# Two transformer blocks in one launch: the Pool engine's two-operand elementwise work moved to VectorE

## Chip, cores and metric

One core of one Trainium2 chip. The metric is the device time of one execution in microseconds (us). Engines are named as the profile names them: PE is TensorE (PEld its weight loads), DVE is VectorE (`V` in the code), ACT is ScalarE (`S`), POOL is GpSimd (`G`, called Pool), SP issues most DMAs.

## The reference

512 tokens of 1024 features in float32 go through two blocks. In outline, cut to what matters (helper functions, reshapes and some arguments are left out):

```python
def first_block(x, mem, ...):
    h = rms_norm(x, norm_mix_pre)
    q_d, k_d, v_d, u_p, q_m, gate_logits = split(h @ w_in)
    y_attn = rms_norm(diff_attention(q_d, k_d, v_d, lam), subln_g) * 0.8 @ w_attn_branch   # 8 heads
    y_pool = multiscale_pool(u_p, ...) @ w_pool_branch    # trailing means over 2, 4, 8, 16 tokens
    y_mem = memory_cross_attention(q_m, rms_norm(mem) @ w_mem_kv) @ w_mem_branch            # 4 heads
    g = sigmoid(gate_logits)
    x = x + rms_norm((g[0] * y_attn + g[1] * y_pool + g[2] * y_mem) @ w_out, norm_mix_post)
    up = causal_depthwise_conv(rms_norm(x, norm_ffn_pre) @ w_up)                            # 3 taps
    return x + rms_norm((gelu(up_g) * up_v) @ w_down, norm_ffn_post)

def second_block(x, c, ctx, c_ctx, ...):                  # 2 layers, context of 256 tokens
    for i in range(2):
        h_lat, h_ctx = (rms_norm(t) * (1 + scale) + shift for t in (x_lat, x_ctx))
        if i == 0:   # attention with rotated, normed heads | attention in a window of 128 with a sink
            y_lat, y_ctx = even_mixer(h_lat, h_ctx, ...)
        else:        # convolution of 31 taps over 512 channels, layer norm | neighbourhood attention, 8 heads
            y_lat, _ = odd_mixer(h_lat, h_ctx, ...)
        x_lat = x_lat + g_l * y_lat                       # and the context in layer 0
    return rms_norm(x_lat, final_g)
```

The change touches the elementwise work around these products: squares for norms, splits of operands, the sums of pool windows and branches, rotations, gates, and the 31-tap convolution of layer 1.

## The kernel before

**Layout.** Activations stand as [128 features, tokens], eight blocks of 512 tokens for the 1024 features. Weights come from memory as tiles `raw` of 128 output features × 1024, two ahead.

**Products.** A float32 product is made of three passes of a reduced type (`mm3`, recorded as L294): high part by high part, high by low, low by high. So each operand needs two parts. For weights `Product.parts` makes them: ACT copies `raw` to `whi` (L458), another engine subtracts, `wlo = raw - whi` (L460). Which engine that is stands in the list `lo_engines`: VectorE, but Pool after `low_parts_on(G)`, which is called at the start (until the first products) and before layer 0's attention. For activations `split` does the same (L489, L490).

**Order.** TensorE works in program order. Products stand in batches; `weave` places steps of a batch between the steps of an attention, `advance` between blocks of a norm. `defer(us, f)` runs f after so many microseconds of products. The list `background` holds work of other engines; `rate[0]` of it is emitted for each microsecond of products, 0.85 in layer 1. The order of the other engines' queues is made by a scheduler from the order of the program and its dependences; each engine works through its queue in order.

**Pool's work before.** Two-operand work: the low parts of weights (above); in `SumSq(..., True)` every third block's square, into an accumulator of its own; in `norm_to` the low part of each block with k % 3 == 1; in `pool_sums` the doubling sums of the windows (L717); in `next_branch` the sum of the mix (L851); in `rotary` two of four products (L1068, L1070); in `post_norm` six of eight x += y (L1418); in `lat_apply` the product by the gate (L1517) and seven of eight splits; in `layer_norm` two sums (L1731, L1732); at the end three of eight last scalings. One-operand work: the scaling of the probabilities by 1/l (L775, L921, L1131), the negation of biases (L1648), fills.

**The convolution of layer 1.** For each of four blocks of channels, `value` forms `up` and puts 32 steps on `background`. Tap 0 is an ACT activation with the bias. Taps 1 to 17 are one VectorE instruction each (L1710), `u = up[j:] * w[j] + u`. The last 13 (`NTAP`) are an ACT activation each that scales (L1713, L1716), and for 12 of them a Pool addition into `ub` (L1717). VectorE adds `ub` to `u` at the end (L1723). The steps of the two kinds alternate. While they run, TensorE works through layer 1's 32 attention steps (`na_items`): scores, minimum (L1122), exponential on ACT (L1126), 1/l on VectorE (L1130), scaling on Pool (L1131), transposes (L586), split on ACT and VectorE (`pth`, `ptl`), output sums (L1163). Products of the next convolution, of attention and of gates are woven in. The layer norm follows the last tap (`layer_norm`: sums over channels, L1736, centring L1741, squares, scaling), beside the products of the gates; the output products follow it.

**Layer 0's attention.** 16 heads of 4 steps, in the same form; in it `lat_apply` applies the gates to finished blocks.

**Norm boundaries.** `post_norm` adds the normed output to x (L1417, L1418) and sums x's squares (L552); `token_sums` makes one matmul for each 128 tokens and accumulator, and `rsqrt` (L524 to L532) works on VectorE.

Of the kernel before, what the change touches and what calls it, by code (L numbers as in the profile page):

```python
# [18 lines left out]
P = 128  # L19
T = 512  # L20
# [4 lines left out]
NTA = 5     # scratch tiles  # L25
NTG = 4     # scratch tiles of the products' results
NRAW = 2    # weight tiles as loaded
NW = 2      # weight tiles in parts
NPT = 1     # transposed probabilities
NSB = {2: 3, 5: 3, 6: 3}     # scores, by the blocks of keys  # L30
NOT = 1     # one half of an attention output
NTAP = 13   # convolution taps on the Pool engine
TH = 3      # last products that take all tokens at once
LL, LN = 2, 2                # heads' scores ahead: latents of layer 0, layer 1

# microseconds of products, or steps of them, before or between other work
SM, SX, SA = 2.4, 4, 8       # start: the memory's root, the input's squares, the input's root
PD = 16                      # multiscale pool
DA, DR, DG = 36, 2.4, 3.7    # differential attention: ahead, for each step, root
B1A = 4                      # second norm of a boundary between layers  # L40
RG = 3.5                     # rotation
MB, CR, MR = 15, 5.4, 0.15   # context: modulation blocks before it, steps, rate of the modulation after it
LA, LR, LZ = 16, 0.5, 1.0    # latents of layer 0: ahead, for each step, fewer after a product
NR = 1.85                    # layer 1: for each step
TD = 2.5                     # last norm

# ---------------------------------------------------------------- host layout
# [135 lines left out]
# ---------------------------------------------------------------- program  # L183


class X:
    """A moving operand in two parts: h and l are [128, kt, n] float32r tiles."""
# [5 lines left out]
class Blocks:  # L193
    """[128, kt, n] as a tile for each of the kt blocks"""
# [8 lines left out]
def body(nc, tc, A, out, dbg=None):  # L203
# [21 lines left out]
    def set_banks(mm, tr, scores=True):  # L225
        """the banks for the products' results and for those of attention and of statistics; scores take four others"""
# [49 lines left out]
    rate = [0.0, 0.0]  # L276
    count = [0]
    woven = []
    lo_engines = deque()

    def low_parts_on(*engines):
        lo_engines.clear()
        lo_engines.extend(engines)
# [1531 lines left out]
```

## Time and profile before

| | |
|---|---|
| three runs | 1807.56, 1810.9, 1818.63 us, median 1810.9 |
| profiled execution, its span | 1808.9 us, 25065 instructions |
| PE busy | 1684.3 us, 93% |
| DVE busy | 1278.4 us, 71%, x2474 |
| ACT busy | 902.7 us, 50% |
| POOL busy | 390.0 us, 22%, x364 |

The profile gives no other time of its execution than the span; it is 2.0 us under the median of the runs. Busy times are shares of that span, and a mean over stages of very different kind: up to 62 us norms and first weights, to 465 the branches' inputs and the two attentions of block 1, to 662 the mix, its output product and the first norm boundary, to 1094 the feed-forward (with the context's attention), to 1150 the second boundary, from 1225 to 1415 layer 0's attention, from 1500 to 1712 layer 1, then the output products and the last norm.

### The profile page before, as it was taken

The page shows a single profiled execution, that of the slowest core. Times are in us where ns is not written, and L with a number is a line of the kernel's source. Part 1 is how long each engine was busy: PE and PEld are TensorE (multiplying, and loading weights), DVE is VectorE, ACT ScalarE, POOL GpSimd, SP SyncE. Part 2 cuts the span into 40 slices and gives each one's busy share as a digit, 9 for nine tenths or more (in the row PEclk, how much of TensorE's full clock was granted, in tenths as well). Part 3 has the DMA queues.
Part 4 walks back from the last instruction along what each step waited for, and adds up shares of the span by engine and source line. Part 5 has one row for each costly group of instructions (what it writes and reads, how often), then busy time and mean ns, then how long its engine had stood idle before and what let it go on. Part 6 is the DMA issues. An engine that isn't in the chain of part 4 may idle for free. (4 is left out here: it accounts for less than half of the span.)

```text
span 1808.9 us, 25065 instructions
## 1 busy us (share of the span) xinstructions
PE 1684.3 (93%) x8756; PEld 1407.0 (78%) x8756; DVE 1278.4 (71%) x2474; ACT 902.7 (50%) x1700; POOL 390.0 (22%) x364
## 2 busy tenths in 40 slices
PE   7899999999998889999999998999988989888797
PEld 7788888888776768888778777778877787777677
DVE  6678766777597676644664767677778667888774
ACT  5443225555423456654763433366767445565452
POOL 3320111010021210000000002145544004656400
PEclk8999999999999999999999999999999999999898
DMA  5435555544364432333333556232321554243141
GB/s 197 136 121 176 162 164 151 135 122 117 126 202 161 148 103 94 123 118 105 111 100 110 193 163 211 84 103 70 78 64 47 186 172 137 82 120 97 35 140 59
DMA packets 84878, 227.10 MB, mean 126 GB/s; under 512 B 12048, under 2 KB 24720, under 8 KB 84752
## 3 DMA queue, kind: packets, MB, share of 16 engines
q1 hardware_dynamic: 82880, 220.51, 39.3%
q10 hardware_dynamic: 1872, 4.98, 0.9%
q8 instruction: 70, 1.15, 0.3%
q14 instruction: 56, 0.46, 0.1%
HBM read 181.93 MB, written 9.44 MB: 106 GB/s over the span
## 5 line engine op out<-in xcount | busy, mean ns | idle before, releaser
L294 PE MATMUL mm<-hh,whi 128*128 128x512 f32 (+1 forms) x1120 | 442.2, 395 | 16.6 <-DVE tg L593 4.6
L458 ACT CAST whi<-raw 128x1024 fp32r<-128x1024 f32 (+2 forms) x264 | 268.4, 1017 | 378.7 <-PE mm L294 326.8
L294 PE MATMUL mm<-hh,wlo 128*128 128x512 f32 (+1 forms) x1120 | 424.1, 379 | 6.4 <-DVE wlo L460 6.4
L294 PE MATMUL mm<-hl,whi 128*128 128x512 f32 (+1 forms) x1120 | 424.5, 379 | 3.4 <-DVE hl L490 1.7
L460 DVE TENSOR_TENSOR wlo<-raw,whi 128x1024 fp32r<-128x1024 f32 (+2 forms) x245 | 309.9, 1265 | 151.1 <-ACT whi L458 147.2
L294 PEld LDWEIGHTS mm<-hh,whi 128*128 128x128 f32 x1120 | 216.6, 193 | 51.4 <-DVE tg L593 6.1
L294 PEld LDWEIGHTS mm<-hh,wlo 128*128 128x128 f32 x1120 | 215.2, 192 | 48.8 <-DVE wlo L460 7.8
L294 PEld LDWEIGHTS mm<-hl,whi 128*128 128x128 f32 x1120 | 216.3, 193 | 34.2 <-DVE hl L997 2.7
L1131 POOL TENSOR_SCALAR sb<-sb,l 128x256 f32<-128x256 f32 (+3 forms) x128 | 106.3, 832 | 453.8 <-DVE l L1130 377.6
L294 PE MATMUL mm<-h2h,whi 128*128 128x512 f32 x352 | 141.8, 403 | 4.0 <-DVE cv L1342 3.0
L490 DVE TENSOR_TENSOR ptl<-tr,pth 128x512 fp32r<-128x512 f32 (+2 forms) x240 | 115.6, 497 | 41.8 <-ACT pth L489 40.0
L489 ACT CAST pth<-tr 128x512 fp32r<-128x512 f32 (+2 forms) x240 | 100.3, 436 | 89.8 <-PE tr L586 88.3
L294 PE MATMUL mm<-h2l,whi 128*128 128x512 f32 x352 | 140.1, 398 | 3.5 <-POOL h2l L490 2.1
L294 PE MATMUL mm<-h2h,wlo 128*128 128x512 f32 x352 | 139.7, 397 | 0.8 <-DVE wlo L460 0.8
L586 PE MATMUL tr<-c,sb 128*128 128x128 f32 x624 | 107.5, 282 | 25.1 <-DVE ptl L490 12.8
L586 PEld LDWEIGHTS tr<-c,sb 128*128 128x128 f32 x624 | 78.9, 145 | 52.0 <-issue 10.3
L810 DVE CUSTOM_DVE_ANT_0 mj<-mraw,cb 128x1024 f32<-128x1024 f32 x88 | 111.1, 1263 | 1.2 <-DMA mraw<-in_mod_w 0.5
L1126 ACT ACTIVATE sb<-sb,mn 128x512 f32<-128x512 f32 (+1 forms) x64 | 49.7, 776 | 70.7 <-DVE mn L1122 51.6
L1710 DVE SCALAR_TENSOR_TENSOR mixf<-up,vec,mixf 128x512 f32<-128x512 f32 x68 | 80.9, 1189 | 1.0 <-ACT mixf L1708 0.2
L294 PEld LDWEIGHTS mm<-h2l,whi 128*128 128x128 f32 x352 | 66.4, 189 | 19.2 <-POOL h2l L490 3.2
L294 PEld LDWEIGHTS mm<-h2h,whi 128*128 128x128 f32 x352 | 66.3, 188 | 19.2 <-issue 4.0
L1717 POOL TENSOR_TENSOR ub<-ub,ta 128x512 f32<-128x512 f32 x48 | 78.9, 1644 | 7.8 <-ACT ta L1716 5.1
(374 smaller groups left out, 3303.6 us busy)
## 6 DMA issues: line engine op xcount, KB each, us to landing
raw<-in_w_in SPq DMA_DIRECT2D x56, 512.0 KB, 3.4
mraw<-in_mod_w SPq DMA_DIRECT2D x48, 512.0 KB, 3.4
raw<-in_w_up SPq DMA_DIRECT2D x44, 512.0 KB, 3.4
raw<-in_ev_w SPq DMA_DIRECT2D x40, 512.0 KB, 3.4
raw<-in_od_w SPq DMA_DIRECT2D x36, 512.0 KB, 3.5
qd<-hl SPq DMA_DIRECT2D x48, 256.0 KB, 5.1
raw<-in_w_d SPq DMA_DIRECT2D x16, 512.0 KB, 3.3
raw<-in_ev_o SPq DMA_DIRECT2D x16, 512.0 KB, 3.4
```

The source lines that it names most:

```text
L294: on_pe(nc.tensor.matmul(ps, l, r, start=start, stop=stop), max(n * 0.00042, 0.107) * (2 if l.dtype == F32 else 1))
L458: S.copy(out=self.hi[:, :n], in_=self.raw[:, :n])
L460: lo_engines[-1].tensor_tensor(out=self.lo[:, :n], in0=self.raw[:, :n], in1=f32(self.hi[:, :n]), op=ALU.subtract)
L489: S.copy(out=hi, in_=src)
L490: (eng or V).tensor_tensor(out=lo, in0=src, in1=f32(hi), op=ALU.subtract)
L586: on_pe(nc.tensor.transpose(out=ps[:, k * P:(k + 1) * P], in_=src(b), identity=ident), 0.107)
L810: tc.keep_in_program_order(V.tensor_tensor_reduce(out=jk, in0=raw, in1=cb[:, n, :], scale=0.5, scalar=0.0, op0=ALU.mult, op1=ALU.add, accu ...
L1126: S.activation(out=sb, in_=src, func=AF.Exp, scale=-1.0, bias=mn, accum_out=l[:, 0:1])
L1131: G.tensor_scalar(out=sb, in0=sb, scalar1=l[:, 0:1], scalar2=0.0, op0=ALU.mult, op1=ALU.add)
L1710: V.scalar_tensor_tensor(out=u[m], in0=up[:, j:j + T], scalar=wc(j), in1=u[m], op0=ALU.mult, op1=ALU.add)
L1717: G.tensor_tensor(out=st["ub"], in0=st["ub"], in1=pj, op=ALU.add)
```

## The change

All two-operand work named above is written for VectorE. Pool keeps the scalings, negations and fills, and gets the copies of at most 8 columns at the head of the pool sums. `SumSq` has one accumulator, so `token_sums` makes four matmuls fewer in each of three norms. The convolution has 30 taps on VectorE for each block of channels (tap 0 stays on ACT), no `ub`, no closing addition, and 31 steps instead of 32 on `background`. At the end the copy of r on ACT goes. Comments go as well, so lines have other numbers after the change (L1710 is L1694, L460 is L451, L490 is L481, L1131 is L1117).

```diff
-                lo_engines.rotate(-1)
-                lo_engines[-1].tensor_tensor(out=self.lo[:, :n], in0=self.raw[:, :n], in1=f32(self.hi[:, :n]), op=ALU.subtract)
+                V.tensor_tensor(out=self.lo[:, :n], in0=self.raw[:, :n], in1=f32(self.hi[:, :n]), op=ALU.subtract)
...
-    def split(src, hi, lo, eng=None):
+    def split(src, hi, lo):
         S.copy(out=hi, in_=src)
-        (eng or V).tensor_tensor(out=lo, in0=src, in1=f32(hi), op=ALU.subtract)
+        V.tensor_tensor(out=lo, in0=src, in1=f32(hi), op=ALU.subtract)
...
-            i = 1 if self.two and self.k % 3 == 2 else 0
-            self.k += 1
-            if i == len(self.accs):
+            if not self.accs:
...
-                (G if i else V).tensor_tensor(out=acc, in0=acc, in1=sq, op=ALU.add)
+                V.tensor_tensor(out=acc, in0=acc, in1=sq, op=ALU.add)
...
-            split(t, dst.h[:, k, :], dst.l[:, k, :], G if k % 3 == 1 else V)
+            split(t, dst.h[:, k, :], dst.l[:, k, :])
...
-    low_parts_on(G)
     advance(filler, SX)
-    ss = SumSq(T, True).add_all(ks(xin))
+    ss = SumSq(T).add_all(ks(xin))
...
-                G.tensor_tensor(out=nx[:, sh:], in0=cur[:, sh:], in1=cur[:, :T - sh], op=ALU.add)
-                V.tensor_copy(out=nx[:, :sh], in_=cur[:, :sh])
+                V.tensor_tensor(out=nx[:, sh:], in0=cur[:, sh:], in1=cur[:, :T - sh], op=ALU.add)
+                G.tensor_copy(out=nx[:, :sh], in_=cur[:, :sh])
...
-        G.tensor_tensor(out=mixacc[:, m, :], in0=mixacc[:, m, :], in1=t, op=ALU.add)
+        V.tensor_tensor(out=mixacc[:, m, :], in0=mixacc[:, m, :], in1=t, op=ALU.add)
...
-                G.tensor_tensor(out=a[1], in0=xf[1], in1=sin, op=ALU.mult)
+                V.tensor_tensor(out=a[1], in0=xf[1], in1=sin, op=ALU.mult)
                 V.tensor_tensor(out=a[2], in0=xf[0], in1=sin, op=ALU.mult)
-                G.tensor_tensor(out=a[3], in0=xf[1], in1=cos, op=ALU.mult)
+                V.tensor_tensor(out=a[3], in0=xf[1], in1=cos, op=ALU.mult)
...
-            (V if k % 4 == 3 else G).tensor_tensor(out=xs[k], in0=xs[k], in1=y[:, k, :], op=ALU.add)
+            V.tensor_tensor(out=xs[k], in0=xs[k], in1=y[:, k, :], op=ALU.add)
...
-        G.tensor_tensor(out=mixf[:, m, :], in0=mixf[:, m, :], in1=sg, op=ALU.mult)
-        defer(2.5, lambda: split(mixf[:, m, :], mix.h[:, m, :], low(m), V if m == 7 else G))
+        V.tensor_tensor(out=mixf[:, m, :], in0=mixf[:, m, :], in1=sg, op=ALU.mult)
+        defer(2.5, lambda: split(mixf[:, m, :], mix.h[:, m, :], low(m)))
...
-    low_parts_on(G)
     set_banks(1, 3)
...
-                elif j < 31 - NTAP:
+                else:
                     V.scalar_tensor_tensor(out=u[m], in0=up[:, j:j + T], scalar=wc(j), in1=u[m], op0=ALU.mult, op1=ALU.add)
-                elif j == 31 - NTAP:
-                    st["ub"] = tl(ep, [P, T], "ub", 1)
-                    S.activation(out=st["ub"], in_=up[:, j:j + T], func=AF.Copy, scale=wc(j))
-                else:
-                    pj = tt()
-                    S.activation(out=pj, in_=up[:, j:j + T], func=AF.Copy, scale=wc(j))
-                    G.tensor_tensor(out=st["ub"], in0=st["ub"], in1=pj, op=ALU.add)
-
-            nv = 31 - NTAP
-            order = [j for a, b in zip(range(nv), chain(range(nv, 31), [None] * 31)) for j in (a, b) if j is not None]
-            order += [j for j in range(31) if j not in order]
-            background.extend([lambda j=j: tap(j) for j in order])
-            background.append(lambda: V.tensor_tensor(out=u[m], in0=u[m], in1=st["ub"], op=ALU.add))
+
+            background.extend([lambda j=j: tap(j) for j in range(31)])
...
-        G.tensor_tensor(out=s1, in0=u[0], in1=u[1], op=ALU.add)
-        G.tensor_tensor(out=s2, in0=u[2], in1=u[3], op=ALU.add)
+        V.tensor_tensor(out=s1, in0=u[0], in1=u[1], op=ALU.add)
+        V.tensor_tensor(out=s2, in0=u[2], in1=u[3], op=ALU.add)
...
-        rs = tl(tmp, [P, T], "sqa", 2)[:, :C]
-        S.copy(out=rs, in_=r)
         for k in range(KD):
             t = tt(C) if k % 2 else tg(C)
-            if k % 3 == 2:
-                G.tensor_tensor(out=t, in0=xs[k][:, cs], in1=rs, op=ALU.mult)
-            else:
-                V.tensor_tensor(out=t, in0=xs[k][:, cs], in1=r, op=ALU.mult)
+            V.tensor_tensor(out=t, in0=xs[k][:, cs], in1=r, op=ALU.mult)
```

Three places show how queues look before and after. Each row is one instruction or several equal ones in a row: line, operation, written tile <- read tiles, shape; tile names are those of the code (`s` scores, `sb` probabilities, `ptl` low part of the transposed ones, `mixf` as target of L1710 or L1694 the convolution's sum).

DVE in layer 1's attention, two steps of one head, before:

```order
L490 TENSOR_TENSOR ptl<-tr,pth 128x128
L1122 ISA sb,mn<-s,nab_13986 128x640
L1122 ISA mn 128x1
L1130 RECIPROCAL l<-l 128x1
L490 TENSOR_TENSOR ptl<-tr,pth 128x2x128 x2
L1122 ISA sb,mn<-s,nab_13986 128x640
L1122 ISA mn 128x1
L1701 SCALAR_TENSOR_TENSOR up<-tg,mm 128x512
```

The same steps after:

```order
L1108 ISA sb,mn<-s,nab_13977 128x640
L1108 ISA mn 128x1
L1694 SCALAR_TENSOR_TENSOR mixf<-up,vec,mixf 128x512
L481 TENSOR_TENSOR ptl<-tr,pth 128x2x128
L1116 RECIPROCAL l<-l 128x1
L1694 SCALAR_TENSOR_TENSOR mixf<-up,vec,mixf 128x512
L481 TENSOR_TENSOR ptl<-tr,pth 128x2x128
L1694 SCALAR_TENSOR_TENSOR mixf<-up,vec,mixf 128x512
L1108 ISA sb,mn<-s,nab_13977 128x640
L1108 ISA mn 128x1
```

Taps now stand between the two splits of a step and between minimum and reciprocal, where none stood. Between the instructions that run from 1517.6 to 1676.4 us in the trace of before stand 96 taps instead of 58.

POOL in layer 0's attention before:

```order
L1131 TENSOR_SCALAR sb<-sb,l 128x512 x2
L1517 TENSOR_TENSOR mixf<-mixf,tg 128x512
L460 TENSOR_TENSOR wlo<-raw,whi 128x1024
L490 TENSOR_TENSOR mixf<-mixf,mixh 128x512
L1131 TENSOR_SCALAR sb<-sb,l 128x640 x2
L1131 TENSOR_SCALAR sb<-sb,l 128x512 x2
```

DVE at the same work after (Pool's queue there holds L1117 alone):

```order
L1149 TENSOR_TENSOR mixf<-tr,ot 64x256
L1503 TENSOR_TENSOR mixf<-mixf,tg 128x512
L481 TENSOR_TENSOR ptl<-tr,pth 128x4x128
L481 TENSOR_TENSOR ptl<-tr,pth 128x2x128
L1106 TENSOR_REDUCE mn<-s 128x1
L481 TENSOR_TENSOR mixf<-mixf,mixh 128x512
L451 TENSOR_TENSOR wlo<-raw,whi 128x1024
L481 TENSOR_TENSOR ptl<-tr,pth 128x4x128
```

The gate's product (L1517, now L1503), the split of the block and a weight's low part have moved from between the scalings into VectorE's queue, between splits of probabilities and a minimum.

DVE at the end of layer 1's attention before:

```order
L1130 RECIPROCAL l<-l 128x1
L1710 SCALAR_TENSOR_TENSOR mixf<-up,vec,mixf 128x512
L1723 TENSOR_TENSOR mixf<-mixf,ub 128x512
L1163 TENSOR_TENSOR mixf<-tr,ot 64x256
L490 TENSOR_TENSOR ptl<-tr,pth 128x4x128
L490 TENSOR_TENSOR ptl<-tr,pth 128x128
```

The same after:

```order
L1116 RECIPROCAL l<-l 128x1
L1694 SCALAR_TENSOR_TENSOR mixf<-up,vec,mixf 128x512
L451 TENSOR_TENSOR wlo<-raw,whi 128x1024
L1149 TENSOR_TENSOR mixf<-tr,ot 64x256
L1694 SCALAR_TENSOR_TENSOR mixf<-up,vec,mixf 128x512
L481 TENSOR_TENSOR ptl<-tr,pth 128x4x128
L481 TENSOR_TENSOR ptl<-tr,pth 128x128
L1694 SCALAR_TENSOR_TENSOR mixf<-up,vec,mixf 128x512
L481 TENSOR_TENSOR ptl<-tr,pth 128x2x128 x2
L1694 SCALAR_TENSOR_TENSOR mixf<-up,vec,mixf 128x512 x3
L1149 TENSOR_TENSOR mixf<-tr,ot 64x256
L1694 SCALAR_TENSOR_TENSOR mixf<-up,vec,mixf 128x512 x3
```

Before, the last tap stands ahead of the last splits; after, nine taps follow the last reciprocal, and six of them the last splits. The layer norm's sums come behind them.

## Rows read from the trace of the kernel before

`mm`, `tr` and `s` are TensorE's results in PSUM; L294 is the matmul helper, L586 the transpose.

**Rows 1.** the page's head: span; busy time, share of the span and instructions
```profile
span 1808.9 us, 25065 instructions
...
PE 1684.3 (93%) x8756; PEld 1407.0 (78%) x8756; DVE 1278.4 (71%) x2474; ACT 902.7 (50%) x1700; POOL 390.0 (22%) x364
```

**Rows 2.** stages: length, PE, PEld, DVE, ACT, POOL busy (instructions), PEclk, DMA share, GB/s
```profile
0.00:62.00 62.00, 46.23 (x286) 42.84 (x287) 42.54 (x76) 31.33 (x58) 23.70 (x16) 0.89 0.58 195
62.00:465.00 403.00, 402.94 (x1987) 334.54 (x1986) 290.82 (x680) 175.06 (x381) 58.12 (x66) 1.00 0.46 137
465.00:558.00 93.00, 87.93 (x373) 69.32 (x371) 78.49 (x121) 28.80 (x46) 15.76 (x8) 0.96 0.56 181
600.00:662.00 62.00, 49.76 (x311) 43.59 (x309) 48.55 (x103) 27.58 (x49) 15.15 (x10) 0.92 0.43 138
662.00:1094.00 432.00, 424.12 (x2049) 348.32 (x2050) 261.02 (x437) 232.91 (x371) 16.04 (x32) 1.00 0.38 123
1094.00:1150.00 56.00, 45.87 (x283) 40.14 (x282) 43.06 (x70) 22.21 (x30) 9.81 (x7) 0.94 0.51 176
1225.00:1415.00 190.00, 170.91 (x1061) 147.58 (x1060) 145.69 (x362) 129.46 (x310) 91.80 (x81) 0.97 0.28 77
1517.60:1676.40 158.80, 139.84 (x723) 113.63 (x721) 143.61 (x205) 95.62 (x181) 104.77 (x86) 0.98 0.36 99
1676.40:1712.00 35.60, 25.74 (x128) 21.02 (x128) 30.70 (x63) 19.45 (x43) 15.66 (x12) 0.78 0.12 42
```

**Rows 3.** PE's waits, 1517.6 to 1676.4: us in total, times, longest
```profile
PE tr L294 <- DVE ptl L490: 8.1, 4, 2.4
PE tr L586 <- DVE mixf L1163: 6.7, 4, 2.1
PE tr L586 <- DVE ptl L490: 2.9, 4, 1.2
```

**Rows 4.** chain of waits in 1517.6 to 1676.4, shares by line
```profile
by line: DVE mixf L1710 31.2%; PE mm L294 22.0%; DVE wlo L460 8.1%; issue 7.7%; DVE ptl L490 4.6%; DVE hl L490 4.4%; DVE sb L1122 3.9%; PE tr L586 3.1%; PE tr L294 3.0%; PE s L294 3.0%; ACT whi L458 1.9%; DVE mixf L1163 1.4%; DVE tg L1672 1
```

**Rows 5.** DVE's groups there: line, engine, out<-in, xcount | busy us, mean ns | idle
```profile
L1710 DVE SCALAR_TENSOR_TENSOR mixf<-up,vec,mixf 128x512 f32<-128x512 f32 x58 | 72.0, 1241 | 1.0 <-ACT mixf L1708 0.2
L460 DVE TENSOR_TENSOR wlo<-raw,whi 128x1024 fp32r<-128x1024 f32 x17 | 23.7, 1394 | 1.3 <-ACT whi L458 1.3
...
L490 DVE TENSOR_TENSOR hl<-tg,hl 128x512 fp32r<-128x512 f32 x3 | 5.3, 1770 | 0.0
```

**Rows 6.** timeline of single instructions there: start us, us, engine, line
```profile
1567.39 5.17 DVE L1710 SCALAR_TENSOR_TENSOR mixf<-up,vec,mixf 128x512 f32<-128x512 f32 x3
1567.31 6.38 POOL L1717 TENSOR_TENSOR ub<-ub,ta 128x512 f32<-128x512 f32 x4
1594.80 0.73 DVE L1710 SCALAR_TENSOR_TENSOR mixf<-up,vec,mixf 128x512 f32<-128x512 f32 x1
1595.78 0.95 DVE L1710 SCALAR_TENSOR_TENSOR mixf<-up,vec,mixf 128x512 f32<-128x512 f32 x1
1595.05 1.15 POOL L1131 TENSOR_SCALAR sb<-sb,l 128x640 f32<-128x640 f32 x1 [4.54 <-DVE l L1130]
```

**Rows 7.** DVE's groups from 662 to 1094, columns as in rows 5
```profile
L460 DVE TENSOR_TENSOR wlo<-raw,whi 128x1024 fp32r<-128x1024 f32 x71 | 86.7, 1222 | 46.9 <-ACT whi L458 44.2 <-PE tr L586 2.6
L552 DVE TENSOR_TENSOR sqa<-sqa,ta 128x512 f32<-128x512 f32 x7 | 4.8, 684 | 0.0
```

**Rows 8.** DVE's groups from 1225 to 1415, columns as in rows 5
```profile
L1125 DVE TENSOR_TENSOR mn<-mn,nsink 128x1 f32<-128x1 f32 x32 | 12.7, 396 | 0.3
...
L1130 DVE RECIPROCAL l<-l 128x1 f32<-128x1 f32 x53 | 8.5, 161 | 8.4 <-ACT sb L1126 6.6 <-POOL mixf L490 1.1
```

**Rows 9.** PE's waits from 1225 to 1415, columns as in rows 3
```profile
PE mm L294 <- DVE tg L593: 4.2, 4, 1.6
PE tr L586 <- POOL sb L1131: 4.2, 3, 1.6
```

**Rows 10.** DVE's group of low parts from 465 to 558, columns as in rows 5
```profile
L460 DVE TENSOR_TENSOR wlo<-raw,whi 128x1024 fp32r<-128x1024 f32 x14 | 25.8, 1845 | 0.5 <-ACT whi L458 0.5
```

More of the change, by code (lines that the diff above doesn't have):

```diff
@@ L31 @@
 NOT = 1
-NTAP = 13
 TH = 3
@@ L278, in body @@
     woven = []
[L279 to L283, printed above, removed]
-    low_parts_on(V)
     def on_pe(ins, us):
@@ L536, in body, with __init__ @@
     class SumSq:
-        def __init__(self, n, two=False, p=None):
-            self.n, self.two, self.p, self.accs, self.k = n, two, p, [], 0
+        def __init__(self, n, p=None):
+            self.n, self.p, self.accs = n, p, []
         def add(self, ap, cols=slice(None)):
-            i = 1 if self.two and self.k % 3 == 2 else 0
-            self.k += 1
-            if i == len(self.accs):
+            if not self.accs:
                 self.accs.append(tl(self.p, [P, self.n], "sqb", 1) if self.p else tl(tmp, [P, T], "sqa", 2)[:, :self.n])
-                S.activation(out=self.accs[i], in_=ap, func=AF.Square)
+                S.activation(out=self.accs[0], in_=ap, func=AF.Square)
             else:
-                sq, acc = tt(ap.shape[-1]), self.accs[i][:, cols]
+                sq, acc = tt(ap.shape[-1]), self.accs[0][:, cols]
                 S.activation(out=sq, in_=ap, func=AF.Square)
-                (G if i else V).tensor_tensor(out=acc, in0=acc, in1=sq, op=ALU.add)
+                V.tensor_tensor(out=acc, in0=acc, in1=sq, op=ALU.add)
             return self
@@ L700, in body @@
     set_banks(2, 2)
-    low_parts_on(V)
     pw = tl(mp, [P, 4, P], "pw", 1)
@@ L1413, in post_norm @@
     def post_norm(y, r, gname, filler, us=0.8):
-        ss = SumSq(T, True)
+        ss = SumSq(T)
         for k in range(KD):
             V.scalar_tensor_tensor(out=y[:, k, :], in0=y[:, k, :], scalar=vc(gname, k), in1=r, op0=ALU.mult, op1=ALU.mult)
-            (V if k % 4 == 3 else G).tensor_tensor(out=xs[k], in0=xs[k], in1=y[:, k, :], op=ALU.add)
+            V.tensor_tensor(out=xs[k], in0=xs[k], in1=y[:, k, :], op=ALU.add)
             advance(filler, us)
@@ L1544, in body @@
     run(filler)
-    low_parts_on(V)
     flush()
```

## Prediction

> **What bounds the kernel now.** The page's head comes first [rows 1]: the span is 1808.9 us and TensorE is busy for 1684.3 of it, so some 125 us are all that any change off TensorE can win. VectorE has 71% and GpSimd (called Pool here) 22%, but these are means, so I cut the span into stages [rows 2]. From 62 to 465 us TensorE is busy for 402.94 of 403.00, from 662 to 1094 for 424.12 of 432.00: work of other engines costs nothing there until it is much more than now. TensorE idles in the start (62.00 − 46.23 = 15.8 us), at the two norm boundaries (12.2 and 10.1), in layer 0's attention (19.1), in layer 1's attention (158.80 − 139.84 = 19.0) and behind it (9.9, at a granted clock of 0.78). These stages decide.
>
> In layer 1's attention VectorE is busy for 143.61 of 158.80 us. TensorE's waits there all name it [rows 3]: the low parts of the probabilities and the sums of the outputs, which stand in VectorE's queue behind the convolution's taps. The chain of waits of that stretch says the same [rows 4]: the taps L1710 make 31.2% of it, 49.5 us, more than the products.
>
> Why VectorE is so full stands in the groups [rows 5] beside single instructions [rows 6]. A tap takes 1241 ns in the mean, but 0.73 us where Pool does nothing. Three taps from 1567.39 take 5.17 us, 1.72 each, beside four Pool additions of 6.38 us. The two engines take turns: a pair of tap and addition costs 1.7 us, as long as two clean taps on VectorE (1.46) and more. So Pool's two-operand work is not free; it is paid on VectorE.
>
> At 1595.05 Pool scales scores by one operand, 1.15 us, and the tap beside it takes 0.95 instead of 0.73: a loss of 0.22.
>
> **What the change returns and adds.** In layer 1's attention: 58 taps × (1.241 − 0.73) = 29.6 us, 17 low parts of weights × (1.394 − 1.222, the clean time from [rows 7]) = 2.9, three splits × (1.770 − 0.68) = 3.3 [rows 5, 7]. That is 35.8 us of VectorE's time, lost beside 45 Pool additions of taps: 0.80 us for each two-operand Pool instruction. I use this price for the other stages.
>
> *Layer 1's attention.* By the order, 96 taps stand on VectorE there instead of 58. Busy time: 143.6 − 35.8 + 38 × 0.73 (27.7) − 3 closing additions of Pool's sum (2.1) = 133.4. Pool keeps 36 one-operand instructions (21 scalings, 15 negations); at 0.22 each they cost 7.9, so at most 141. TensorE needs 139.84. The taps are now spread through all items, where before VectorE was full beside some and half idle beside others. At best both engines fit into TensorE's own time: −19. At worst VectorE, still nearly full, holds up TensorE in as many places as now: 0. I take −10, the middle, since 133 to 141 us of VectorE against 140 of TensorE leave neither engine much slack.
>
> *Behind it, 1676.4 to 1712.* Fourteen taps more, 24 for 10, are 10.2 us, less 1.5 for the last closing addition and one price: +9 if all of it delays the layer norm's sums, which wait for the last tap. Nothing if it hides: TensorE is busy for 25.74 of 35.60 us there, with products of the gates that need no tap, and nine taps stand behind the last scores, beside these. I take +3, a third, since only the first of the taps there share the queue with splits for which TensorE waits.
>
> *Layer 0's attention.* VectorE gets 9 low parts × 1.222 and 19 other operations (8 gate products, 7 splits, 4 rotations) × 0.68: 23.9 us on 145.69 busy of 190. By the price 28 × 0.80 = 22.4 come back. What one can point to is less: 32 minima of one column take 396 ns, where a reciprocal of one column takes 161, so 7.5 us [rows 8]. So VectorE gains between 1.5 and 16 us of work, with 44 free. TensorE's waits for Pool's scaled scores (4.2 us) go, since no low part of a weight stands ahead of a scaling; its waits for VectorE (4.2 for the gates, and smaller ones) [rows 9] grow. Bounds −4 (nothing but the Pool wait) and +11; I take 0.
>
> *The start.* Seven low parts and four sums come to VectorE: 7 × 1.222 + 4 × 0.68 = 11.3, against 11 × 0.80 = 8.8. VectorE is busy for 42.54 of 62 us, so the 2.5 are partly hidden: +1 (−2 to +4).
>
> *The attention branch, 465 to 558.* Fourteen low parts take 1845 ns there [rows 10], 14 × 0.62 = 8.7 us lost beside eight additions of the mix, which cost 8 × 0.68 = 5.4 on VectorE. TensorE's idle 5 us bound it: −2 (−5 to +1).
>
> *The norm boundaries.* Seventeen operations, returned at 13.6, added at 11.6; four matmuls fewer in each sum over tokens. But x += y and the squares now stand in one queue with the weights' low parts: −1 (−5 to +6).
>
> *Elsewhere nothing.* Rotations ahead of layer 0's attention cost 0.68 and return 0.80 each. The pool's window sums and the memory's branches lie in the stretch where TensorE is full. The small copies that go to Pool lie there too; their cover is that same full stretch, and it is VectorE's 112 free microseconds in it (403 − 290.82) that would have to be used up before they cost anything.
>
> *The end.* The last scalings no longer wait for a copy on ScalarE: I put nothing, it is below half a microsecond by the few instructions in it.
>
> Sum: −10 + 3 + 0 + 1 − 2 − 1 = −9. The profiled execution has 1808.9; the median of the three runs, 1810.9, stands 2.0 above. 1808.9 − 9 + 2 = 1802.
>
> **A rule beside it.** The loss of a tap beside a scaling is 0.22 us in the row [rows 6]. The Trainium skill, page "SBUF — State Buffer", section "Who interferes with whom", says that a VectorE instruction with two inputs in SBUF contends with any GpSimd instruction that reads SBUF, and that the one that comes second waits until the first has ended. The pairs of taps and additions agree with it, 1.72 us each; the single 0.95 does so only if the scaling was nearly over. By that rule the one-operand work that stays would cost more than I counted, which is the second rival.
>
> **The rivals.**
> *All of it comes back.* VectorE falls below TensorE in layer 1 and the waits of [rows 3] go as a whole (−19), the taps behind it hide (0), layer 0 loses its waits for Pool (−4). For it: 133 us against 139.84. Against it: a wait in program order needs only a local queue. 1810.9 − 19 − 4 + 1 − 2 − 1 = 1786.
> *The rest of Pool's work blocks as much.* Each of 36 one-operand instructions in layer 1 holds up a tap by half of its own 1.15 us, 0.58, instead of 0.22: 20.9 us instead of 7.9. VectorE then has 154 us of work again and TensorE waits as before: term 0 instead of −10, so 1812. For it: Pool's queue gets empty, so each scaling starts at once, in the midst of taps. Against it: the row with 0.95.
> *The queue decides, not the sum.* VectorE works in order, and in both attention stages each operation added to it stands ahead of a minimum or a split for which TensorE waits; none hides. In layer 0 all 23.9 us then land, and 4 of Pool's waits go: +20. In layer 1 the 38 taps more are 27.7 us, and only the stretch of those taps that lie on the chain of waits comes back, 49.5 × (1.241 − 0.73) / 1.241 = 20.4: +7. With the other terms as forecast, 1810.9 + 20 + 7 + 3 + 1 − 2 − 1 = 1839. It decides once TensorE's waits for VectorE pass 30 us in the one stage or 25 in the other, where they are 17.7 in [rows 3]. For it: the taps now stand between the steps of every item, and in layer 0 only 7.5 us of stretch can be pointed to. Against it: 44 us of VectorE are free there, and scores run ahead of their use by two items.
> That the change leaves work on Pool is no case: in the order no two-operand instruction stands there any more.
>
> **How the numbers follow.** Chances: forecast 0.50 (its own range 1791 to 1813), all back 0.17, rest blocks 0.15, queue 0.18. A measurement here tells about 1% from no change, so the marks are 1792.8 and 1829. The first rival and 0.10 from the forecast's lower edge give faster 0.27; the third gives slower 0.17, nearly all of its case; the rest, 0.56, is the same. The range 1780 to 1832 takes in the first two rivals and leaves out most of the third.
>
> **What would show it.** Right: taps near 0.75 to 0.85 us in layer 1; VectorE busy for 133 to 141 us in that stretch, TensorE idle for under 12; low parts of weights at 1.22 between 465 and 558. Wrong: taps still above 0.9 (the second rival); TensorE's waits for VectorE above 30 us in layer 0 or 25 in layer 1 (the third); or the wait for the layer norm's sums ahead of the last products, which would say that the tail decides.

## The result, and the profile after

The kernel after took 1789.76 us in the median of four runs (1787.08 to 1791.94), the kernel before 1809.23 (1806.27 to 1818.63): a ratio of 0.9889, 95% interval 0.9865 to 0.9912. It is faster by 1.1%, 19.5 us. The forecast was 1802, with a range of 1780 to 1832; the time lies in the range, on the side of its first rival, and the gain is more than twice the 9 us of the sum.

The head of the page of after answers to [rows 1]:

```profile
span 1790.1 us, 24872 instructions
...
PE 1675.1 (94%) x8732; PEld 1404.5 (78%) x8732; DVE 1283.6 (72%) x2612; ACT 869.9 (49%) x1646; POOL 167.6 (9%) x229
```

Pool lost 222 us of work, and VectorE's busy time grew by only 5 us, from 1278.4 to 1283.6, though it took over all of Pool's two-operand instructions. Nearly as much came back as was added. But a sum over the span does not tell where the 18.8 us between the two spans went. For that I laid the two traces side by side by TensorE's instructions, whose order is the same but for twelve matmuls that went (24 in the page's count) and a few steps, and noted how far the same matmul lies later or earlier after the change:

| stage of before | forecast | shift within the stage |
|---|---|---|
| start, 0 to 62 us | +1 | +1.8 |
| 62 to 465 | 0 | 0.0 |
| attention branch and output product, 465 to 600 | −2 | −3.2 |
| first norm boundary, 600 to 662 | −1 for both boundaries | +3.3 |
| feed-forward, 662 to 1094 | 0 | −0.6 |
| second boundary, 1094 to 1150 | (see above) | +3.0 |
| rotations, 1150 to 1225 | 0 | +1.2 |
| layer 0's attention, 1225 to 1415 | 0 | −2.3 |
| its output product, layer 1's head, 1415 to 1517.6 | 0 | +3.0 |
| layer 1's attention, 1517.6 to 1676.4 | −10 | −24.0 |
| behind it, 1676.4 to 1712 | +3 | 0.0 |
| the rest, to the end | 0 | −1.0 |
| sum | −9 | −18.8 |

So one stage gave more than the whole, and the others together took 5 back. (The row's end at 1676.4 falls between two matmuls; by the next one layer 1's attention has −25.0 and the stretch behind it +1.1.) The stages of after, cut at the same instructions, answer to [rows 2] (length, then busy times of PE, PEld, DVE, ACT, POOL, granted clock, DMA share, GB/s):

```profile
0.00:63.80 63.80, 45.44 (x278) 42.37 (x279) 41.11 (x88) 31.90 (x58) 0.30 (x5) 0.89 0.57 193
...
466.80:561.30 94.50, 89.09 (x379) 70.60 (x378) 77.10 (x135) 30.33 (x48) 0.00 (x0) 0.96 0.55 179
598.60:663.80 65.20, 49.60 (x302) 44.57 (x301) 49.81 (x115) 27.59 (x49) 0.00 (x0) 0.84 0.41 129
...
1095.30:1154.30 59.00, 47.35 (x274) 40.91 (x274) 43.96 (x78) 22.25 (x30) 0.00 (x0) 0.88 0.49 167
...
1229.60:1418.20 188.60, 172.06 (x1066) 148.05 (x1065) 155.07 (x392) 128.46 (x312) 47.87 (x54) 0.97 0.30 82
...
1523.80:1658.60 134.80, 132.79 (x719) 111.30 (x718) 133.54 (x243) 67.61 (x134) 38.32 (x40) 1.00 0.41 116
1658.60:1694.00 35.40, 24.08 (x133) 20.12 (x132) 34.38 (x70) 17.04 (x39) 9.10 (x7) 0.87 0.12 41
```

Layer 1's attention went from 158.80 to 134.80 us. VectorE is busy for 133.54 of these, where before it had 143.61 with 38 taps fewer. Its groups there show why (columns as in [rows 5], which they answer to):

```profile
L1694 DVE SCALAR_TENSOR_TENSOR mixf<-up,vec,mixf 128x512 f32<-128x512 f32 x96 | 74.6, 777 | 0.7
L451 DVE TENSOR_TENSOR wlo<-raw,whi 128x1024 fp32r<-128x1024 f32 x17 | 20.8, 1223 | 0.0
...
L481 DVE TENSOR_TENSOR hl<-tg,hl 128x512 fp32r<-128x512 f32 x3 | 2.0, 681 | 0.0
```

A tap takes 777 ns instead of 1241, so 96 taps take 74.6 us, where 58 took 72.0. Low parts and splits are back at their clean 1.22 and 0.68. Of TensorE's three lines of waits in [rows 3], 17.7 us, one of 1.8 is left in that stretch (a fourth line of before, 1.0 us for ScalarE, which the prediction passes over, is gone too):

```profile
PE tr L574 <- DVE ptl L481: 1.8, 2, 1.4
```

The stretch's chain of waits still names the taps, more than in [rows 4]:

```profile
by line: DVE mixf L1694 41.1%; PE mm L286 10.9%; DVE wlo L451 9.0%; issue 8.7%; DVE sb L1108 8.1%; DVE ptl L481 7.0%; DVE mixf L1149 2.4%; DVE hl L481 2.3%; PE tr L286 1.7%; PE s L286 1.6%; PE tr L574 1.3%; DVE l L1116 1.1%; DVE vt L1021 0.
```

That is to be read with care. 41.1% of 134.8 us is 55 us, and VectorE is idle for only 1.3 us, but TensorE is busy for 132.79 of 134.80 as well. A chain picks one of two full engines; which of them binds is asked of an experiment below.

### The profile page after: what moved, and what is told of

The parts are those of the page before. It is cut to its first block, busy times and chain, and to the rows that moved or that the text cites. A ratio compares the mean times of both kernels' runs of the same rounds, so it can differ in the third digit from the quotient of the medians.

```text
span 1790.1 us, 24872 instructions
## 1 busy us (share of the span) xinstructions
PE 1675.1 (94%) x8732; PEld 1404.5 (78%) x8732; DVE 1283.6 (72%) x2612; ACT 869.9 (49%) x1646; POOL 167.6 (9%) x229
## 5 line engine op out<-in xcount | busy, mean ns | idle before, releaser
L451 DVE TENSOR_TENSOR wlo<-raw,whi 128x1024 fp32r<-128x1024 f32 (+2 forms) x264 | 311.9, 1182 | 158.4 <-ACT whi L450 154.9
L1117 POOL TENSOR_SCALAR sb<-sb,l 128x256 f32<-128x256 f32 (+3 forms) x128 | 111.1, 868 | 985.0 <-DVE l L1116 613.6
L480 ACT CAST pth<-tr 128x512 fp32r<-128x512 f32 (+2 forms) x240 | 101.0, 436 | 104.3 <-PE tr L574 102.7
L481 DVE TENSOR_TENSOR ptl<-tr,pth 128x512 fp32r<-128x512 f32 (+2 forms) x240 | 116.1, 497 | 31.8 <-ACT pth L480 30.3
L574 PE MATMUL tr<-c,sb 128*128 128x128 f32 x624 | 105.3, 278 | 19.5 <-DVE ptl L481 11.7
L796 DVE CUSTOM_DVE_ANT_0 mj<-mraw,cb 128x1024 f32<-128x1024 f32 x88 | 107.8, 1225 | 2.0 <-DMA mraw<-in_mod_w 1.3
L1694 DVE SCALAR_TENSOR_TENSOR mixf<-up,vec,mixf 128x512 f32<-128x512 f32 x120 | 93.2, 777 | 0.9
L286 PEld LDWEIGHTS mm<-h2h,wlo 128*128 128x128 f32 x352 | 66.5, 189 | 17.5 <-DVE wlo L451 1.5
L286 PE MATMUL s<-kp,qd 128*128 128x256 f32 (+3 forms) x320 | 76.7, 337 | 0.7 <-ACT sb L1112 0.7
```

The source lines that it names most:

```text
L286: on_pe(nc.tensor.matmul(ps, l, r, start=start, stop=stop), max(n * 0.00042, 0.107) * (2 if l.dtype == F32 else 1))
L451: V.tensor_tensor(out=self.lo[:, :n], in0=self.raw[:, :n], in1=f32(self.hi[:, :n]), op=ALU.subtract)
L480: S.copy(out=hi, in_=src)
L481: V.tensor_tensor(out=lo, in0=src, in1=f32(hi), op=ALU.subtract)
L574: on_pe(nc.tensor.transpose(out=ps[:, k * P:(k + 1) * P], in_=src(b), identity=ident), 0.107)
L796: tc.keep_in_program_order(V.tensor_tensor_reduce(out=jk, in0=raw, in1=cb[:, n, :], scale=0.5, scalar=0.0, op0=ALU.mult, op1=ALU.add, accu ...
```

## The experiments

Intervals are of the ratio to the kernel before on the same chip; "after" stands at 0.9889 on its first chip. Where a stage is quoted, it is cut at the same TensorE instructions as above.

**The convolution alone, and all the rest alone.** The first kernel takes the convolution's lines of the change, and no others, into before (cut here: the lines of ScalarE's and Pool's taps go, and the layer norm's second sum moves as the first does):

```diff
-                elif j < 31 - NTAP:
+                else:
                     V.scalar_tensor_tensor(out=u[m], in0=up[:, j:j + T], scalar=wc(j), in1=u[m], op0=ALU.mult, op1=ALU.add)
...
+            background.extend([lambda j=j: tap(j) for j in range(31)])
...
-        G.tensor_tensor(out=s1, in0=u[0], in1=u[1], op=ALU.add)
+        V.tensor_tensor(out=s1, in0=u[0], in1=u[1], op=ALU.add)
```

> The kernel before with one part of the change: the convolution's 30 taps and the two sums of its layer norm on VectorE. Theory A (the gain is the time that VectorE loses beside Pool's additions of taps, and the rest of the change together loses some 6 us ahead of layer 1): 1785 us, 24 under before, with taps near 0.78 us. Rival B (every part of the change returns its share of the same price): half of the gain or less, 1797 to 1800. In both Pool does its other two-operand work as before.

The second undoes just these lines in after.

> The kernel after with the convolution and its layer norm's sums as before (13 taps by ScalarE and Pool). Theory A: slower than before by the losses seen ahead of layer 1, 1813 to 1815 us, and taps at 1.2 us again. Rival B: faster than before, 1798 to 1802, since low parts, sums and gate products returned their share.

The convolution alone took 1785.43 us against 1806.54, ratio 0.9885 (0.9859 to 0.9911): the whole gain of the change. The rest alone took 1809.94, ratio 1.0019 (1.0003 to 1.0036): 3.4 us slower, if anything. Rival B falls, theory A stands, with smaller losses than the 6 it gave. The groups of taps, of the convolution alone and of the rest alone:

```profile
L1710 DVE SCALAR_TENSOR_TENSOR mixf<-up,vec,mixf 128x512 f32<-128x512 f32 x95 | 74.6, 785 | 0.7
```

```profile
L1695 DVE SCALAR_TENSOR_TENSOR mixf<-up,vec,mixf 128x512 f32<-128x512 f32 x58 | 71.9, 1239 | 1.0 <-ACT mixf L1693 0.2
```

Layer 1's attention is the same in each kernel with the same convolution: 24.5 us shorter in the first, 0.1 longer in the second.

**What about the convolution: Pool's company, ScalarE's scalings, or the taps' spreading?** Three kernels add back to after what went, without its effect on the result. At the steps j = 18 to 30 of each block of channels:

```diff
+            def extra(j):
+                if j == 18:
+                    st["ub"] = tl(ep, [P, T], "ub", 1)
+                    S.activation(out=st["ub"], in_=up[:, j:j + T], func=AF.Copy, scale=wc(j))
+                elif j > 18:
+                    G.tensor_tensor(out=st["ub"], in0=st["ub"], in1=up[:, j:j + T], op=ALU.add)
...
-            background.extend([lambda j=j: tap(j) for j in range(31)])
+            background.extend([lambda j=j: (tap(j), extra(j)) for j in range(31)])
```

> The kernel after with 48 additions of two operands (128x512) put on Pool at the steps of the convolution where before had its own, into a tile that nothing reads (a ScalarE copy fills it first, one for each block of channels). The convolution itself stays on VectorE. Theory A (the price is the company of a two-operand instruction on Pool, whatever it is for): 48 x 0.80 = 38 us come back onto VectorE, which has no slack in layer 1's attention, so 30 to 38 us over after, and taps at 1.1 us. Rival B (the gain came from ScalarE's scalings that went, from one step less in the list or from taps that are spread more evenly): at most 3 us over after, taps under 0.85.

In the second, Pool's line is `G.tensor_scalar(out=st["ub"], in0=st["ub"], scalar1=wc(j), scalar2=0.0, op0=ALU.mult, op1=ALU.add)`.

> The same with 48 one-operand instructions on Pool (each scales that tile in place, 128x512, by one column). Row theory (a tap loses little beside a one-operand instruction: 0.08 to 0.22 us): 4 to 10 us over after. Rule of the Trainium skill, page SBUF — State Buffer, section Who interferes with whom (any Pool instruction that reads SBUF contends with a VectorE instruction of two SBUF inputs, and the second waits): about what the two-operand additions cost, 25 us or more over after.

In the third, it is the ScalarE copy of j == 18 again.

> The kernel after with 52 scaled copies on ScalarE at those steps (128x512, into a tile that nothing reads), as before had them for its Pool additions; Pool gets nothing. Theory A: ScalarE has 67 of 135 us busy in layer 1's attention and can take 33 more: 0 to 2 us over after. Rival B (ScalarE's share of the taps delayed the exponentials and splits): 5 to 12 us over after.

With the two-operand additions the time was 1817.29 us, ratio 1.0025 (1.0005 to 1.0046), so 1.0025 − 0.9889 = 1.4% or 25 us over after; against the kernel with ScalarE's copies, which ran on the same chip, it is 27.9 us. Layer 1's attention grew by 25.7 us, the stretch behind it by 3.9. With the one-operand instructions it was 1798.95 us, ratio 0.9934 (0.9912 to 0.9956), 0.45% or 8 us over after; the stage grew by 7.2 and the stretch behind it by 1.7. With ScalarE's copies it was 1789.35 us, ratio 0.9883 (0.9856 to 0.9909), no difference; the stage grew by 1.2, within the 0 to 2 of theory A. The stage, its taps and Pool's added instructions, with the additions:

```profile
1521.80:1682.30 160.50, 141.65 (x718) 115.32 (x716) 159.72 (x239) 69.71 (x139) 107.53 (x84) 0.96 0.34 97
```

```profile
L1694 DVE SCALAR_TENSOR_TENSOR mixf<-up,vec,mixf 128x512 f32<-128x512 f32 x95 | 94.4, 994 | 0.6
```

```profile
L1702 POOL TENSOR_TENSOR ub<-ub,up 128x512 f32<-128x512 f32 x44 | 68.2, 1549 | 6.9 <-ACT ub L1700 4.3
```

with the one-operand instructions:

```profile
1522.10:1664.10 142.00, 134.63 (x719) 111.47 (x717) 141.22 (x241) 69.50 (x139) 85.83 (x83) 1.00 0.39 110
```

```profile
L1694 DVE SCALAR_TENSOR_TENSOR mixf<-up,vec,mixf 128x512 f32<-128x512 f32 x96 | 80.0, 834 | 0.6
```

```profile
L1702 POOL TENSOR_SCALAR ub<-ub,vec 128x512 f32<-128x512 f32 x44 | 49.9, 1135 | 7.5 <-ACT ub L1700 4.3
```

and with ScalarE's copies:

```profile
1521.40:1657.40 136.00, 133.18 (x718) 111.58 (x717) 134.76 (x241) 97.61 (x182) 35.69 (x40) 1.00 0.41 116
```

ScalarE's 30 us more (97.61 against 67.61) cost nothing that a time shows. VectorE's busy time is the measure of the company: 159.72 − 133.54 = 26.2 us for 44 additions of Pool within the stage, 0.60 each, and 141.22 − 133.54 = 7.7 us for 44 one-operand instructions, 0.17 each. Theory A's mechanism stands, with the price a quarter under the 0.80 it gave, so that the time came out below its 30 to 38 us. Rival B falls. That the scalings of probabilities stand behind additions in Pool's queue is not the cause either: none of the waits of TensorE that the profile lists in the stage with the additions names Pool, and the second kernel puts three quarters as much work into that queue (49.9 us against 68.2) for three tenths of the loss. What falls too is the Trainium skill's rule as I had read it for this test (page "SBUF — State Buffer", section "Who interferes with whom"): it makes no difference between Pool instructions that read one operand and those that read two, and the run shows a factor of 3.4 between them (26.2 against 7.7 us). That Pool's one-operand work disturbs VectorE at all agrees with it: the 0.17 is not zero.

**Which engine binds layer 1 now?** The taps 23 to 30 are left out:

```diff
-            background.extend([lambda j=j: tap(j) for j in range(31)])
+            background.extend([lambda j=j: tap(j) if j < 23 else None for j in range(31)])
```

> The kernel after without the last 8 of 31 taps of each block of channels (32 VectorE instructions are left out, some 26 of them in layer 1's attention; the convolution's result lacks them). If VectorE alone now sets that stretch (133.54 of 134.80 us busy): 26 x 0.78 = 20 us less there. If TensorE is as full (132.79 of 134.80): 2 to 5 us less there, and 2 to 4 less behind it, where the layer norm's sums wait for the last tap.

```profile
1515.20:1647.10 131.90, 131.90 (x718) 111.80 (x717) 122.48 (x224) 68.83 (x137) 35.67 (x41) 1.00 0.42 122
1647.10:1680.50 33.40, 23.43 (x132) 19.67 (x131) 29.32 (x60) 15.99 (x37) 5.86 (x6) 0.91 0.10 32
```

The stage is 2.9 us shorter than in after, though VectorE has 11 us less to do. TensorE is now busy for all of 131.90: its floor, which after misses by 2.9 us. The stretch behind it, 35.40 us in after, is 2.0 shorter; of the 24 taps there 11 are left out. Both are as expected of a TensorE that is as full as VectorE. So the two engines are full together in after, and eight taps of each block of channels less on VectorE are worth these five microseconds and not the 16 by which VectorE's busy time fell. The time of the run, ratio 0.9829 (0.9802 to 0.9855), is not the measure: 8.7 us of the profile's 13.9 lie ahead of layer 1, where the two kernels have the same instructions, in stages that wait for loads.

**The norms and the late root.** Two kernels took up the losses ahead of layer 1. In the first, the start and the norm boundaries work as before: low parts of weights at the start on Pool, `SumSq(T, True)`, six of eight x += y and the low part of every third block on Pool, the rest as after.

> The kernel after with the norms' work as before: low parts of weights at the start on Pool, squares in two accumulators, six of eight x += y and the low parts of every third block on Pool. Theory A (in these short stages VectorE's single queue is what TensorE waits for, and two queues are better in spite of the price): the start's 1.8, the first boundary's 3.2 and the second's 3.0 us come back, 1782 us. Rival B (the price paid there is as large as the work moved): 1790, no difference.

The second changes only the estimate of time by which `defer` places work. The sum over tokens has four matmuls fewer since there is one accumulator, so `clock` counts 4 × 0.214 = 0.86 us less:

```diff
             y = rsqrt(token_sums(self.accs, self.n), dim, e)
+            clock[0] += self.more
+            rate[1] += self.more * rate[0]
             advance(filler, 2.9)
...
+        ss.more = 0.856
         return ss.add(xs[-1])
```

> The kernel after, in which the four matmuls that each sum over tokens no longer issues are still counted (0.86 us) in the estimate by which deferred work is placed; TensorE's order is then that of before but for those matmuls. Theory A (at the first boundary the loss comes from a root's spreading that fell due later and now stands behind eight blocks of the norm on VectorE: one wait of 6.94 us): that wait falls to 2 us or less and the time to 1785. Rival B (the loss there is VectorE's added work): the wait moves but the time stays at 1789 to 1790.

They took 1780.45 us, ratio 0.9857 (0.9832 to 0.9883), and 1785.7 us, ratio 0.9882 (0.9858 to 0.9906). On another chip than after such differences can't be told apart, so both ran again, beside after itself, and beside after with layer 0's part on Pool:

> The kernel after, unchanged, on the same chip as the three that follow, so that few microseconds can be compared: 0.989 of before. Its stages tell how far two profiles of equal instructions differ: layer 1's attention again 134 to 136 us, the stages bound by loads (the start, 465 to 560) within 3 us.

> The kernel after with the norms' work on Pool as before (start, both boundaries), again. Theory A (two queues are better there): 5 to 8 us under after on this chip. Rival B (the first comparison was over two chips and the differences are those of the load-bound stages): within 2 us of after.

> The kernel after with the four matmuls still counted in the estimate that places deferred work, again. Theory A (the late root at the first boundary costs): 2 to 4 us under after, the stage from 600 to 662 shorter by 2.6. Rival B: no difference in time, within 1 us.

> The kernel after with layer 0's attention as before: nine low parts of weights, eight gate products and seven splits on Pool again. If the move was neutral there (the forecast's 0): within 2 us of after. If it won what the trace of after shows (2.3 us shorter): 2 to 3 us over after, with TensorE waiting for Pool's scaled scores again for 4 us.

| kernel, one chip | median us | ratio | interval |
|---|---|---|---|
| after | 1786.92 | 0.9865 | 0.9831 to 0.9899 |
| norms on Pool | 1781.74 | 0.9831 | 0.9799 to 0.9863 |
| due time | 1786.34 | 0.9858 | 0.9827 to 0.9890 |
| layer 0's part on Pool | 1788.65 | 0.9876 | 0.9840 to 0.9912 |

After came out at 134 to 136 us for layer 1's attention again, and no stage differs by more than 1.6 us from the first profile of it. In the kernel with taps left out, stages with equal instructions differed by up to 3.4 (465 to 560 us, which waits for loads). Between these two lies what a stage of one profile can tell here. All fourteen profiles together tell more; they stand at the end of this section.

The wait that the late root caused is plain in the trace. TensorE's longest wait in the first boundary, in after (636 to 656 us) and with the due time mended (632 to 654):

```profile
PE tr L286 <- DVE ta L504: 6.9, 1, 6.9
```

```profile
PE tr L286 <- DVE ta L504: 1.6, 1, 1.6
```

With one accumulator less, the estimate ran 0.86 us behind, the spreading of a root of the context's keys (L504, 0.28 us of work) fell due after the whole norm of eight blocks instead of inside it, and in VectorE's queue it stood behind the last of them. The mended order is that of before; the stage, cut as in the first table, is 2.5 us shorter than in after in this profile and 2.6 in the first. The time shows no difference (1786.34 against 1786.92, within the 1 us of rival B), so theory A is shown for the wait and its stage, and not for the whole.

The norms on Pool ran under after both times they were measured, by 5.2 us on the same chip, though the intervals overlap; in the profile the start is 1.8, the first boundary 2.9 and the second 2.7 us shorter than in after. It is the fastest version of this study that computes the whole result, and it keeps the convolution on VectorE. That two queues are better there is likely, and in the first boundary the late root, which returns to its place as well, accounts for most of it. The second boundary has no such root, and so speaks for the queues.

Layer 0's part on Pool took 1.7 us more than after in time, which the intervals do not tell from nothing, and 1.7 in the stage. Expected were 2 to 3 or nothing. The stage does decide, once all profiles are laid side by side: it is 187.2 to 187.6 us long in ten of the eleven with that part on VectorE. These are the lengths of five stages in all fourteen profiles, each cut at the same matmuls:

| stage of before | its work on Pool, as before | its work on VectorE |
|---|---|---|
| start | 60.2 to 62.2 (4 profiles) | 61.2 to 64.5 (10) |
| first norm boundary | 62.2 to 63.8 (4) | 65.4 to 66.1 (7), once 64.0; with the due time mended 62.8 and 63.0 |
| second boundary | 56.0 to 57.1 (4) | 57.9 to 59.6 (10) |
| rotations, 1150 to 1225 | 75.0 (2) | 76.2 to 76.3 (11), once 77.6 |
| layer 0's attention | 189.3 to 192.6 (3) | 187.2 to 187.6 (10), once 189.2 |

So the loss at the second boundary, a small loss at the rotations and a gain of about 2 us in layer 0 are clear of the spread; the loss at the start is not.

## Why the prediction was right, and where it was not

The time lies in the range in part by errors that went opposite ways: layer 1's attention gave 14 us more than forecast, and the other stages together took 4 more.

**Layer 1's attention (forecast −10, measured −24).** The mechanism was right, the size was not, and the measured value lies outside the term's own bounds, −19 to 0. The first half of the step held to a tenth of a microsecond: VectorE's busy time was put at 133.4 and came out at 133.54. So close a meeting is in part luck: the taps lost 3.4 us beside Pool's one-operand work, which the 133.4 left out, and the sum laid instructions end to end, where the records of successive ones overlap (in after a split from 1639.49 us takes 0.68, and the tap behind it starts at 1640.09). The 7.9 us for the one-operand work were too much: 96 × (0.777 − 0.742) is the 3.4, as the 70 of the run's 120 taps beside which Pool does nothing take 742 ns.

The step that failed is "TensorE needs 139.84", from which the floor of −19 and the caution about "little slack" came. That number is busy time in a stretch with waits, and holds more than the products need. The granted clock was 0.98: in two stretches of 3.4 us, at 1536 and 1628 us, each at waits of TensorE of 1.9 to 2.3 us, it stood at the lower level, 1.2 GHz (0.50). Matched matmul by matmul, those in these stretches took 3.0 us more than in after, and those right behind a wait 2.2 more. The same products are busy for 132.79 at a clock of 1.00 in after, 131.90 without a wait when taps are left out, 141.65 at 0.96 with Pool's additions put back, and 143.82 at 0.95 in the kernel with the rest alone, which has before's convolution and before's length:

```profile
1520.10:1679.00 158.90, 143.82 (x723) 117.56 (x721) 143.78 (x205) 95.66 (x181) 105.11 (x86) 0.95 0.36 99
```

TensorE took 4 us more than in before there and the stage 0.1 us, because VectorE, which the waits name, set its length. So the stage could give 158.80 − 131.90 = 26.9, and gave 24.0: 17 us of idle time (19.0 to 2.0) and 7 of busy time. (For the same reason the 125 us that the prediction took for the most that any change off TensorE can win are not a limit: TensorE's own busy time fell by 9 us over the span, most of it here.) VectorE was the bound before, and the middle between the bounds was the wrong place to stand, since an engine that falls from 143.6 to 133.4 us of work takes the stage with it.

**Behind it (+3, measured 0.0 to +1.1 by where it is cut).** Most of the taps there hide, but not all: with 11 of them left out the stretch was 2.0 us shorter.

**The uniform price, 0.80.** Measured alone it is 0.60 for a two-operand Pool instruction in layer 1. What it gave for layer 0, 22.4 us returned, was far off: the busy time of VectorE rose there from 145.69 to 155.07, by 9.4 of the 23.9 us that came, so that 14.5 returned. The part that could be pointed to was real; the minima of one column fell from 396 ns in [rows 8] to the length of any one-column operation, 32 × 0.239 = 7.6 us against the 7.5 of the text:

```profile
L1111 DVE TENSOR_TENSOR mn<-mn,nsink 128x1 f32<-128x1 f32 x32 | 5.0, 157 | 0.2
```

**Layer 0's attention (0, measured −2.3).** The size was near, but one reason was wrong. "TensorE's waits for Pool's scaled scores (4.2 us) go" did not come true; the wait of [rows 9] is there as before, though no low part of a weight stands in Pool's queue:

```profile
PE tr L574 <- POOL sb L1117: 5.0, 6, 1.5
PE mm L286 <- DVE tg L581: 4.3, 4, 1.4
```

The scalings themselves are longer beside VectorE's added work (last section). The waits for VectorE did not grow to the 30 us of the third rival; the largest is the 4.3 shown. What gave the 2 us stays open.

**The attention branch (−2, measured −3.2 with the output product).** Its low parts fell from 1845 ns in [rows 10] to the clean time, as said:

```profile
L451 DVE TENSOR_TENSOR wlo<-raw,whi 128x1024 fp32r<-128x1024 f32 x15 | 18.2, 1216 | 0.0
```

**The start (+1, measured +1.8)** came out near the forecast, in a stage whose profiles spread by 3 us.

**1150 to 1225 (nothing forecast, +1.2).** Six rotation products and three low parts of weights moved to VectorE here. "Cost 0.68 and return 0.80 each" would have made that a gain; the loss is small, and all twelve profiles show it. No run tells the two kinds of work apart.

**The norm boundaries (−1, measured +6.3, just beyond the upper bound of +6).** "Returned at 13.6, added at 11.6" is a sum of busy time, and these stages are chains, in which order decides. The late root is 2.5 of the 3.3 us at the first boundary. I had counted the four matmuls that go as a gain and not looked at what else their time set: the due times of the work behind them.

**1415 to 1517.6 (nothing forecast, +3.0).** None of the changed lines is executed there. The fourteen profiles have 101.9 to 105.7 us in that stretch, before 102.7, and the first profile of after is the longest of all; the second is 1.1 shorter. So at least part of the +3.0 is spread; the rest stays open.

**The rivals.** "All of it comes back" (1786) is the nearest, wrong in its −4 for layer 0 and right in that layer 1's waits went, but for 1.8 us. The second, that Pool's one-operand work blocks as much, fell with taps of 777 ns and with the run that doubled that work. The third, the queue, is found at the norm boundaries and at neither place where it was put.

## What to carry to other kernels

Where two engines slow each other down, price a move by the stretch that the trace shows on the engine that binds its stage, and test that price with dummy work that leaves the result alone. Do not take the busy time of an engine that waits as its floor: a stage without waits shows less, as TensorE's 131.90 against 139.84 us did here. And when an estimate of time places the work, an instruction that goes moves what falls due behind it; look for such a root before calling the edit a gain.

## What the runs showed of the hardware

**The company costs both sides, and mostly Pool where its work has one operand.** Pool's scaling of 640 columns took 803 ns in the mean in layer 0 before and 879 after, with VectorE's added work. In layer 1, where VectorE was fuller from the start, it took 1111 before and 1255 after. Negating 256 columns went from 472 ns in layer 1 before to 960. (Spans on Pool are rough in the profile; the second profile of after has 1254 and 937 in layer 1.) The rows, of layer 0 and then of layer 1, first before and then after:

```profile
L1131 POOL TENSOR_SCALAR sb<-sb,l 128x640 f32<-128x640 f32 x16 | 12.8, 803 | 24.9 <-DVE l L1130 17.5 <-DVE l L1129 4.5 <-ACT ot L1162 1.4
```

```profile
L1117 POOL TENSOR_SCALAR sb<-sb,l 128x640 f32<-128x640 f32 x16 | 14.1, 879 | 42.5 <-DVE l L1116 19.4 <-ACT pth L480 8.2 <-DVE mn L1111 6.1
```

```profile
L1131 POOL TENSOR_SCALAR sb<-sb,l 128x640 f32<-128x640 f32 x10 | 11.1, 1111 | 23.2 <-DVE l L1130 21.8 <-ACT ta L1716 1.3
...
L1648 POOL TENSOR_SCALAR nab<-nab 128x256 f32<-128x256 f32 x10 | 4.7, 472 | 5.3 <-DMA nab<-in_nab 5.2
```

```profile
L1117 POOL TENSOR_SCALAR sb<-sb,l 128x640 f32<-128x640 f32 x10 | 12.6, 1255 | 30.5 <-DVE l L1116 13.6 <-ACT pth L480 7.5 <-PE s L286 6.5
...
L1632 POOL TENSOR_SCALAR nab<-nab 128x256 f32<-128x256 f32 x10 | 9.6, 960 | 1.7 <-DMA nab<-in_nab 1.6
```

A tap loses 0.035 us in the mean in layer 1 after. VectorE's gain is so paid for in part by Pool, which has the time in layer 1 and not quite in layer 0.

**Even operations on one column are held up**: the minima of one column in layer 0 stood at 396 ns in the mean beside Pool's two-operand work and at 157 without it. The mean hides how: of the 48 in the whole run before, 41 took at most 0.16 us, and seven took 0.48 to 2.06.
